# Other step orders for nine units of a Strassen-scheduled decoder block, and a branch sum joined by accumulating transfers

## The chip, the cores and the metric

The kernel runs on one core of a Trainium2 chip. The metric is the time of the kernel on the device, in microseconds, over whole executions; lower is better. A core has a matrix engine (PE), a vector engine (DVE), a scalar engine (ACT), GpSimd (POOL) and SyncE (SP). Each engine works through its own instructions in order, and engines wait for one another by semaphores. SP issues the weight loads, POOL the transfers of everything else; in a row of the profile SPq and POOLq are the queues of these transfers.

## The reference

The input x has 256 tokens of 4096 channels, everything is float32, and one block is computed. Cut to what matters:

```python
h = rmsnorm(x, norm_w)
proj = h @ w_in                        # 4096 -> six parts of 2048 and 8192 gate logits
u_p, z_p, u_c, b_c, c_c, z_c, g_logit = split(proj)
y_pool = pool(u_p, pool_w, pool_scale) * silu(z_p)
y_conv = b_c * shortconv(c_c * u_c, conv_w, conv_b) * silu(z_c)
br = [y_pool @ w_branch[0], y_conv @ w_branch[1]]     # 2048 -> 4096 each
gates = sigmoid(g_logit + gate_b)                     # 2 x 4096
x = x + (gates[0] * br[0] + gates[1] * br[1]) @ w_out # 4096 -> 4096
out = rmsnorm(x, final_norm_w)
```

`pool` takes four groups of 512 channels; each is averaged over a trailing window of 2, 4, 8 or 16 tokens, the token itself is subtracted, and the result is multiplied with a 512 x 512 matrix of its group ("mixing"). `shortconv` is a causal convolution over three tokens.

## The kernel before

**Units and steps.** The outputs of the large products are cut into units of 1024 columns. A unit runs over the rows of its weight matrix in steps of 256 rows by 1024 columns, 1 MB each: 16 steps in an input or output unit, 8 in a branch unit. Every float32 product is made from three passes over values split in a high and a low part (high x high, high x low, low x high). A step is one of two kinds. A direct step ("P") multiplies the four 128-row, 512-column pieces with both halves of the tokens: 24 matmuls of 128 x 512. A Strassen step ("S") makes seven products instead of eight from sums of the pieces: 21 matmuls, in seven groups of three, and needs more of DVE, since it forms four sums of the weights (`parts`) and splits them too. The products of a direct step go into the four banks of PSUM that are called `sums`; those of a Strassen step go into `sums` and the four banks called `shared`. The order of the kinds in a unit is written out as a string (`SEVEN5` is the name of such a string with 7 S, the direct steps first).

**Preparing a step.** SP loads the weights into one of three buffers `raw`. ACT rounds them to high parts, DVE subtracts to get low parts; both go into cells of a `ring` of 15 cells of 512 columns. For a Strassen step DVE first forms the sums in `parts`, which are then split in the same way. Preparation runs up to `AHEAD = 4` steps ahead of PE as the cells come free. In the code, `Step.first` and `Step.rest` issue it, `pump` decides when. A Strassen step is `closing` when it ends its unit; it then fills the banks `sums` in its first three groups and the banks `shared` in the other four.

**The end of a unit.** When a bank is complete, ACT copies it: `evacuate` takes a bank of `sums` into the tile E (Y in some units), `copy_corners` takes a bank of `shared` into J. `corner_sums` combines the four parts of J on DVE, and `combine` adds J to E. It does so on DVE (L61, or L73 with the scale of the norm in `rin`), or, in a unit with `late` set, by two transfers of POOL that accumulate in memory (`gather`, L85); the scale is then applied later. After that comes the unit's epilogue, a list of functions and gaps in a queue. One entry is taken at each "tick", which is every 6 matmuls; `gap(n)` are n ticks without work. So an epilogue runs in the first third of the next unit, between its matmuls, and the engines see its instructions in the place where the tick emitted them.

**The order of units.** cz, cb, cu, cc (the four conv inputs, for c = 0 and then c = 1), pz0, pu0, pz1, pu1 (the pool inputs), eight gate units g0_0, g0_1, g1_1, g0_2, g1_2, g0_3, g1_3, g1_0, then b0_0, b1_0, b0_1, b1_1 and so on to b1_3 (branch units n and c: branch n, columns c), and the outputs o0 to o3. pz1 and g0_0 are hosts: the letter B in their string stands for the step that multiplies the pool input just computed (pu0, pu1) with two band matrices, and M for one group's mixing. In these two units the string `HOST` sets where that stands among their own 16 steps. The epilogues of pu0 and pu1 are empty: E goes into the B step.

**Branch units.** `branch_unit` builds them. b0_c is the pool branch; its result E is multiplied into Y (which holds the first gate) by `mul(Y, E, Y)` during b1_c. In the epilogue of b1_c, which runs during the next b0, E is multiplied with the second gate (`spare()`, the tile `last_pair`), Y is added, and PE transposes the sum (L458) for the output stage. Their left operands, eight of branch 0 and eight of branch 1, lie in `arena` in regions that `place` gives out: four blocks per part for a direct step's operand, seven or eight for a Strassen one's. They are brought in by POOL and split (`Fill`) while the units before run, as regions come free.

Of the kernel before, what the change touches and what calls it, by code (L numbers as in the profile page):

```python
# [10 lines left out]
F32R = mybir.dt.float32r  # L11
# [4 lines left out]
P = 128  # L16
T = 256
D = 4096
HALF = D // 2
NU = 1024  # L20
# [3 lines left out]
KB = 256  # L24

ND, NS, NB = 8, 6, 2
# [5 lines left out]
TAIL = 3  # L32

SIX5 = "PPPPPSPSPSPSPSPS"
SEVEN5 = "PPPPPSPSSPSPSSPS"
FIRST = (0, 1, 8, 2, 9, 3, 10, 11, 4, 12, 13, 5, 14, 6, 15, 7)
OPENED = 12
SEVEN3 = "PPPSPSPSPSPSPSPS"
NINE = "PSPSPSPSSPSPSSPS"
NINE_A = "PSPSSPSPSSPSPSPS"  # L40
HOST = "PPPBPPMMPSPSSPSSPSS"
TEN = "PSPSSPSSPSSPSSPS"
OUT3 = "PSPSPSPSPSPSSPPP"
B0 = "PPPPSPSP"
B1 = "PSPSPSPP"
B1_FIRST = "PPSPSPSP"
B1_LAST = "PSPPSPPP"


@with_exitstack  # L50
def hybrid_block(ctx: ExitStack, tc: tile.TileContext, x, xc, prm, rows_in, w_in, pool_w, w_branch, w_out, out):
    nc = tc.nc
# [4 lines left out]
    def act(dst, src, func=AF.Copy, **kw):  # L57
        return pin(nc.scalar.activation(dst, src, func, **kw))  # L58

    def tt(dst, a, b, op):  # L60
        return pin(nc.vector.tensor_tensor(out=dst, in0=a, in1=b, op=op))  # L61

    def mul(dst, a, b):
        return tt(dst, a, b, ALU.mult)
# [7 lines left out]
    def stt(dst, a, s, b, op0, op1, **kw):  # L72
        return pin(nc.vector.scalar_tensor_tensor(out=dst, in0=a, scalar=s, in1=b, op0=op0, op1=op1, **kw))  # L73
# [7 lines left out]
    def move(dst, src):  # L81
        return pin(nc.gpsimd.dma_start(dst, src))
# [10 lines left out]
    def sb(name, shape, dt=F32):  # L93
        return upper.tile(shape, dt, name=name)

    def blocks(name, shape, dt=F32):
        return const.tile(shape, dt, name=name)

    blocks("front", [P, 96])
    arena = blocks("arena", [P, (4 * ND + 7 * NS + 8 * (NB - 1)) * KB], F32R)  # L100
    ring = blocks("ring", [P, CELLS, 2, NH], F32R)
    E = blocks("E", [P, 2, NU])
    sa = blocks("sa", [P, 8, P])
# [3 lines left out]
    Y = sb("Y", [P, 2, NU])  # L107
# [10 lines left out]
    gates_d = dram.tile([2, 4, P, 2, NU], F32, name="gates_d")  # L118
# [14 lines left out]
    def bias_col(b):  # L133
        return par[:, 80 + b:81 + b]
# [26 lines left out]
    def place(region):  # L161
        kind, i = region
        if kind == "p":
            return 4 * KB * i, 4
        if kind == "q":
            return (4 * ND + 14 + 4 * i) * KB, 4
        if i < NS:
            return (4 * ND + 7 * i) * KB, 7
        return (4 * ND + 7 * NS + 8 * (i - NS)) * KB, 8
# [227 lines left out]
    def shared(i):  # L397
        return PF[i]
# [52 lines left out]
    def transposes(src, done):  # L451
        items = []
        for j in range(4):
            def f(j=j):
                for i in range(2):
                    for t in range(2):
                        c = (2 * j + i) * P
                        pin(nc.tensor.transpose(shared(j)[:, i * T + t * P:i * T + (t + 1) * P],  # L458
                                                src[:, t, c:c + P], ident))
                done(j)  # L460
            items.append(f)
        return items

    def pairs(items):
        return [lambda a=a, b=b: (a(), b()) for a, b in zip(items[::2], items[1::2])]
# [5 lines left out]
    def chan(tile_):  # L471
        return tile_.rearrange("p a n -> p (a n)").rearrange("p (b t) -> p b t", t=T)
# [4 lines left out]
    def gap(n):  # L477
        return [None] * n
# [5 lines left out]
    def make_ops(kinds):  # L484
        return [Operand(k, r) for k, r in kinds]

    x_ops = make_ops([("P" if r[0] == "p" else "S", r) for r in x_regions])
    y_ops = [make_ops([("P", ("p", i)) for i in range(6)] + [("S", ("s", i)) for i in (0, 1)]),
             make_ops([("P", r) for r in (("p", 6), ("p", 7), ("q", 0), ("q", 1), ("q", 2))] +
                      [("S", ("s", i)) for i in (6, 4, 5)])]  # L490
    m_ops = make_ops([("P" if r[0] == "p" else "S", r) for r in x_regions])

    def sequence(text, np_, total, both):
# [24 lines left out]
    def in_unit(name, col, epi, text, **kw):  # L518
        units.append(Unit(name, lambda i: w_in[col // NU, i], seq_x(text), x_ops, epi, scaled=True, **kw))
        units[-1].text = text  # L520
        return units[-1]
# [15 lines left out]
    def silu_y(late):  # L537
        def silu(t):
            act(Y[:, t], Y[:, t], AF.Silu, **(dict(scale=rin[:, t:t + 1]) if late else {}))
        return gap(18 if late else 3) + [lambda: silu(0), None, lambda: silu(1)]  # L540
# [5 lines left out]
    def conv_units(c, first):  # L546
        base = 2 * HALF + c * NU

        def b_epi(u):
            def product(t):  # L550
                stt(E[:, t], E[:, t], rin[:, t:t + 1], Y[:, t], ALU.mult, ALU.mult)
            return gap(18) + [lambda: product(0), None, lambda: product(1), None, lambda: move(g_d[c], E)]

        def c_epi(u):
            def inner(j):
                if j == 3:
                    for i in range(4):
                        act(chan(E)[:, 2 * i:2 * i + 2], bankview(i))

            def outer(j):  # L560
                act(chan(J)[:, 2 * j:2 * j + 2], bankview(j))

            def taps(j):
                v, y = chan(E)[:, 2 * j:2 * j + 2], chan(Y)
                for i in range(2):
                    b = 2 * j + i
                    kb = 8 * c + b
                    act(y[:, b], v[:, i], AF.Identity, scale=tap_col(2, kb), bias=bias_col(kb))
                for s in (1, 2):
                    for i in range(2):  # L570
                        b = 2 * j + i
                        kb = 8 * c + b
                        stt(y[:, b, s:], v[:, i, 0:T - s], tap_col(2 - s, kb), y[:, b, s:], ALU.mult, ALU.add)

            items = [lambda: move(Y, g_d[c])] + gap(6) + pairs(transposes(E, inner)) + gap(5) + pairs(transposes(Y, outer))
            for j, n in enumerate((1, 7, 8, 8)):
                items += gap(n) + [lambda j=j: taps(j)]
            return items + [None, lambda: mul(chan(E), chan(J), chan(Y)), lambda: put(y_d[1, c], chan(E))]

        u = in_unit(f"cz{c}", base + 3 * HALF, lambda u: silu_y(u.late) + (gap(4) + side_items(ND - 1) + side_items(ND - 2) if first else []),  # L580
                    FIRST if first else SEVEN5, dst=Y)
        u.late = not first
        in_unit(f"cb{c}", base + HALF, b_epi, TEN if c else NINE_A).late = True
        u = in_unit(f"cu{c}", base, lambda u: rescale(Y), NINE, dst=Y)
        u.late = True
        in_unit(f"cc{c}", base + 2 * HALF, c_epi, NINE_A).urgent = lambda: mul(E, E, Y)

    def pool_units(c):
        u = in_unit(f"pz{c}", HALF + c * NU, lambda u: silu_y(True) + gap(4) + band_items(c), HOST if c else SEVEN5, dst=Y)
        u.late = True  # L590
        in_unit(f"pu{c}", c * NU, lambda u: [], NINE).urgent = lambda: None

    def band_items(c):
        if c == 0:
# [92 lines left out]
    def gate_unit(n, c):  # L687
        first, final = (n, c) == (0, 0), (n, c) == (1, 0)

        def epi(u):  # L690
# [10 lines left out]
            return items if first or final else items + [lambda: move(gates_d[n, c], E)]  # L701
        text = HOST if first else SEVEN3 if final else TEN
        u = in_unit(f"g{n}_{c}", 6 * HALF + n * D + c * NU, epi, text, dst=Y if first else E)
        u.late = not final

    def spare():
        return last_pair["tile"].rearrange("p (a n) -> p a n", a=2)

    def branch_unit(n, c):
        def epi(u):  # L710
            if n == 0:
                return gap(8) + [lambda: mul(Y, E, Y), None, lambda: c and move(spare(), gates_d[1, c])]
            turned = spare() if c < 3 else Y

            def gated():
                mul(E, E, spare())
                if c == 3:
                    last_pair["stack"].close()
                    open_last(F32R)
                    last_pair["again"] = True  # L720

            def copy(j):
                act(chan(turned)[:, 2 * j:2 * j + 2], bankview(j))

            def stored():
                put(m_d[c], chan(turned))
                merged[c] = now[0] + STORED
            return gap(2) + [gated, None, lambda: add(E, E, Y), None,
                lambda: c < 3 and move(Y, gates_d[0, c + 1])] + gap(3) + pairs(transposes(E, copy)) + [stored]

        text = (B1_LAST if c == 3 else B1 if c else B1_FIRST) if n else B0
        u = Unit(f"b{n}_{c}", lambda i: w_branch[n, c, i], seq_y(text), y_ops[n], epi)
        u.urgent, u.lead = (lambda: None), 3
        units.append(u)

    merged = {}
# [224 lines left out]
    def done(i):  # L961
        steps[i].prepared = True
# [276 lines left out]
```

## Time and profile before

| | |
|---|---|
| runs, median (lowest, highest) | 2361.7 us (2361.68, 2362.04) |
| the profiled execution's own time | 2362.3 us |
| its span in the trace | 2360.3 us |
| granted PE clock in it | 0.999 |
| matmuls; weight loads | 10,436; 10,436 |
| DVE, ACT, POOL instructions | 2430, 1832, 189 |
| moved by transfers | 566.28 MB, mean 240 GB/s |

The span runs from the first to the last instruction of the trace; the execution's own time is 2.0 us longer. The page's busy line gives, for each engine, the time in which it executed something, its share of the span and its instructions; register, branch and DMA-issuing instructions are not in it. PE's ends are modelled, and matmuls overlap, so a stretch in which PE is busy throughout can still hold matmuls that came a little late. For that reason lengths of single steps are read as well: a step begins with its first matmul and ends where the next one begins. Numbers in names (`sums_82`) are of PSUM banks.

### The profile page before, as it was taken

What the parts mean: (1) busy time and instruction counts of PE and PEld (TensorE: products, weight loads), DVE (VectorE), ACT (ScalarE), POOL (GpSimd) and SP (SyncE); (2) the same over time, 40 slices, a digit from 0 to 9 for tenths busy, and PEclk for the clock granted to TensorE, in tenths of its full rate; (3) what the DMA queues carried; (4) which work ended last, traced back from release to release, by engine and by line L of the source; (5) the groups of instructions that cost most, each with busy time, mean ns of one, the idle gap of its engine ahead of it and who ended that gap; (6) DMA issues with size and microseconds to landing.
All of it is one profiled execution on the core that took longest, in us unless ns stands there. A gap on an engine that the chain in (4) does not pass through costs nothing.

```text
span 2360.3 us, 28303 instructions
## 1 busy us (share of the span) xinstructions
PE 2344.8 (99%) x10436; PEld 1939.8 (82%) x10436; DVE 2206.1 (93%) x2430; ACT 1535.1 (65%) x1832; POOL 131.3 (6%) x189
## 2 busy tenths in 40 slices
PE   9999999999999999999999999999999999999998
PEld 7888888888888888888888888888888888888886
DVE  8899989999979979979999999999998798899998
ACT  6666656666666666656767767766665566566665
POOL 0000000000001100100000000001100001000000
PEclk9999999999999999999999999999999999999999
DMA  9667655776756656656887787778766657667877
GB/s 349 234 233 245 221 202 202 253 232 237 230 197 210 235 181 223 231 187 217 253 261 246 259 262 249 249 261 287 250 221 245 251 212 258 245 210 267 259 254 280
DMA packets 93754, 566.28 MB, mean 240 GB/s; under 512 B 10225, under 2 KB 10481, under 8 KB 33201
## 3 DMA queue, kind: packets, MB, share of 16 engines
q1 hardware_dynamic: 69824, 485.39, 56.7%
q0 software_dynamic: 23216, 77.87, 12.9%
q8 instruction: 81, 1.33, 0.2%
q10 hardware_dynamic: 576, 1.24, 0.1%
q14 instruction: 57, 0.46, 0.1%
HBM read 521.46 MB, written 25.17 MB: 232 GB/s over the span
## 4 chain that ended last, share of the span: by engine, by line
PE 93%; DVE 4%; DMA 1%; issue 1%; ACT 1%; SPq 0%; DVEq 0%; ACTq 0%
PE sums L1018 67%; PE shared L1018 24%; DVE ring L61 2%; DVE parts L61 1%; PE shared L672 1%; DMA raw<-in_w_in_dram 1%; PE shared L458 1%; DVE E L61 1%; ACT ring L58 0%; DVE Y L73 0%; DVE J L61 0%; PE shared L648 0%; ACT J L58 0%; DVE E L73 0%; ACT E L58 0%
## 5 line engine op out<-in xcount | busy, mean ns | idle before, releaser
L1018 PE MATMUL sums<-ring,arena 128*128 128x512 f32 x7041 | 1648.4, 390 | 2.5 <-ACT E L58 0.9
L1018 PEld LDWEIGHTS sums<-ring,arena 128*128 128x128 f32 x7041 | 1320.1, 188 | 279.0 <-ACT E L58 2.2
L61 DVE TENSOR_TENSOR ring<-raw,ring 128x1024 fp32r<-128x1024 f32 (+3 forms) x884 | 964.4, 1110 | 92.9 <-ACT ring L58 91.5
L58 ACT ACTIVATE ring<-raw 128x1024 fp32r<-128x1024 f32 (+3 forms) x685 | 787.9, 1190 | 199.9 <-PE sums L1018 79.3
L58 ACT ACTIVATE ring<-parts 128x512 fp32r<-128x512 f32 (+1 forms) x669 | 502.0, 762 | 520.2 <-DVE parts L61 461.4
L1018 PE MATMUL shared<-ring,arena 128*128 128x512 f32 x2217 | 535.4, 389 | 0.0
L61 DVE TENSOR_TENSOR ring<-parts,ring 128x1024 fp32r<-128x1024 f32 (+1 forms) x465 | 515.3, 1150 | 2.9 <-ACT ring L58 2.8
L1018 PEld LDWEIGHTS shared<-ring,arena 128*128 128x128 f32 x2217 | 416.1, 188 | 86.5
L61 DVE TENSOR_TENSOR parts<-parts,raw 128x512 f32<-128x512 f32 x436 | 297.6, 683 | 0.0
L61 DVE TENSOR_TENSOR parts<-raw 128x1024 f32<-128x1024 f32 x218 | 265.2, 1217 | 11.5 <-DMA raw<-in_w_in_dram 6.3
L61 DVE TENSOR_TENSOR J<-J 128x512 f32<-128x512 f32 (+1 forms) x90 | 78.1, 867 | 8.8 <-ACT J L58 6.2
L1018 PE MATMUL sums<-ring,last_pair 128*128 128x512 f32 x336 | 83.0, 389 | 0.0
L1018 PEld LDWEIGHTS sums<-ring,last_pair 128*128 128x128 f32 x336 | 63.0, 188 | 13.2 <-DVE ring L61 0.2
L58 ACT ACTIVATE J<-shared 128x512 f32<-128x512 f32 x128 | 69.1, 603 | 2.2 <-PE shared L1018 0.9
L85 POOL DMA_DIRECT2D E<-J x22 | 26.8, 1459 | 431.3 <-ACT ring L58 315.5
L1018 PE MATMUL shared<-ring,side 128*128 128x512 f32 x207 | 50.7, 389 | 0.0
L1018 PE MATMUL shared<-ring,last_pair 128*128 128x512 f32 x192 | 46.1, 389 | 0.0
L1018 PEld LDWEIGHTS shared<-ring,side 128*128 128x128 f32 x207 | 38.9, 188 | 8.1
L58 ACT ACTIVATE E<-sums 128x512 f32<-128x512 f32 x76 | 42.0, 596 | 4.0 <-PE sums L1018 1.8
L1018 PEld LDWEIGHTS shared<-ring,last_pair 128*128 128x128 f32 x192 | 36.0, 188 | 7.5
L85 POOL DMA_DIRECT2D Y<-J x12 | 14.7, 1455 | 247.6 <-issue 121.7
L672 PE MATMUL shared<-ring 128*128 128x512 f32 x96 | 22.1, 389 | 0.0
(140 smaller groups left out, 639.3 us busy)
## 6 DMA issues: line engine op xcount, KB each, us to landing
raw<-in_w_in_dram SPq DMA_DIRECT2D x318, 1024.0 KB, 4.9
raw<-in_w_branch_dram SPq DMA_DIRECT2D x64, 1024.0 KB, 4.8
raw<-in_w_out_dram SPq DMA_DIRECT2D x64, 1024.0 KB, 5.1
E<-J POOLq DMA_DIRECT2D x22, 512.0 KB, 8.8
E<-in_rows_dram POOLq DMA_DIRECT2D x14, 512.0 KB, 9.6
Y<-J POOLq DMA_DIRECT2D x12, 512.0 KB, 9.7
gates_d<-E POOLq DMA_DIRECT2D x6, 1024.0 KB, 6.2
y_d<-E POOLq DMA_DIRECT2D x8, 512.0 KB, 7.7
```

What stands on the lines that cost most here:

```text
L58: return pin(nc.scalar.activation(dst, src, func, **kw))
L61: return pin(nc.vector.tensor_tensor(out=dst, in0=a, in1=b, op=op))
L85: return pin(nc.gpsimd.dma_start(dst, src, accum_op=ALU.add))
L458: pin(nc.tensor.transpose(shared(j)[:, i * T + t * P:i * T + (t + 1) * P], src[:, t, c:c + P], ident))
L672: pin(nc.tensor.matmul(o, a, b, start=(k, i) == (0, 0), stop=(k, i) == (3, 2)))
L1018: pin(nc.tensor.matmul(ps, lhs, rhs, start=n == 0, stop=n == u.total[b] - 1))
```

## The change

- **Fewer Strassen steps in cz1 and pz0.** They take `SIX5` (six S) instead of `SEVEN5` (seven).
- **Hosts.** `HOST` has one S more, and B stands one step earlier, behind two direct steps instead of three.
- **pu0 and pu1.** A new string `NINE_P` with the same nine S, but a direct step at the end.
- **Branch units.** b0_1, b0_2 and b0_3 take `B0_MORE` with three S instead of two, and close with one. They become `late`: the sum E + J is made by POOL's transfers instead of DVE, and they lose the rule by which their last step holds back preparation (`lead`). Their epilogue waits longer: `mul(Y, E, Y)` comes 19 ticks into b1 instead of 8, and the load of the second gate, which stood behind it, stands 10 ticks in. b1_3 takes `B1` (three S) instead of `B1_LAST` (two). b0_0 keeps `B0`, b1_0 keeps `B1_FIRST`.
- **Transposes.** In the epilogues of b1_0 to b1_2 the gap before them is 4 instead of 3.
- **Room.** The branch operands get other regions (`place` has two more kinds), since one more of each branch is held as a Strassen operand; `arena` grows by two blocks, and the scratch memory for the descriptors of POOL's transfers is halved.

```diff
-SEVEN5 = "PPPPPSPSSPSPSSPS"
...
+NINE_P = "PSPSSPSPSSPSSPSP"
-HOST = "PPPBPPMMPSPSSPSSPSS"
+HOST = "PPBPPMMPSSPSSPSSPSS"
...
-B1_LAST = "PSPPSPPP"
+B0_MORE = "PPPPSSPS"
...
-    arena = blocks("arena", [P, (4 * ND + 7 * NS + 8 * (NB - 1)) * KB], F32R)
+    arena = blocks("arena", [P, (4 * ND + 7 * NS + 8 * (NB - 1) + 2) * KB], F32R)
...
-    y_ops = [make_ops([("P", ("p", i)) for i in range(6)] + [("S", ("s", i)) for i in (0, 1)]),
-             make_ops([("P", r) for r in (("p", 6), ("p", 7), ("q", 0), ("q", 1), ("q", 2))] +
-                      [("S", ("s", i)) for i in (6, 4, 5)])]
+    y_ops = [make_ops([("P", ("p", i)) for i in range(5)] + [("S", r) for r in (("t", 0), ("s", 0), ("s", 1))]),
+             make_ops([("P", r) for r in (("p", 7), ("q", 0), ("q", 1), ("q", 2), ("q", 3))] +
+                      [("S", ("u", i)) for i in (2, 0, 1)])]
...
-                    FIRST if first else SEVEN5, dst=Y)
+                    FIRST if first else SIX5, dst=Y)
...
-        u = in_unit(f"pz{c}", HALF + c * NU, lambda u: silu_y(True) + gap(4) + band_items(c), HOST if c else SEVEN5, dst=Y)
+        u = in_unit(f"pz{c}", HALF + c * NU, lambda u: silu_y(True) + gap(4) + band_items(c), HOST if c else SIX5, dst=Y)
         u.late = True
-        in_unit(f"pu{c}", c * NU, lambda u: [], NINE).urgent = lambda: None
+        in_unit(f"pu{c}", c * NU, lambda u: [], NINE_P).urgent = lambda: None
...
             if n == 0:
-                return gap(8) + [lambda: mul(Y, E, Y), None, lambda: c and move(spare(), gates_d[1, c])]
+                if c:
+                    return gap(10) + [lambda: move(spare(), gates_d[1, c])] + gap(8) + [lambda: mul(Y, E, Y)]
+                return gap(8) + [lambda: mul(Y, E, Y)]
...
-                lambda: c < 3 and move(Y, gates_d[0, c + 1])] + gap(3) + pairs(transposes(E, copy)) + [stored]
-
-        text = (B1_LAST if c == 3 else B1 if c else B1_FIRST) if n else B0
+                lambda: c < 3 and move(Y, gates_d[0, c + 1])] + gap(4) + pairs(transposes(E, copy)) + [stored]
+
+        text = (B1 if c else B1_FIRST) if n else B0_MORE if c else B0
...
-        u.urgent, u.lead = (lambda: None), 3
+        u.late = n == 0 and c > 0
+        if not u.late:
+            u.urgent, u.lead = (lambda: None), 3
...
-    nc = _bacc.Bacc("TRN2", target_bir_lowering=False, num_devices=1, dynamic_dma_scratch_size=4096)
+    nc = _bacc.Bacc("TRN2", target_bir_lowering=False, num_devices=1, dynamic_dma_scratch_size=2048)
```

The first place is DVE at the end of cz1, from the last sums of its last but one Strassen step to the first step of the next unit. `parts<-raw` begins a Strassen step, `ring<-parts` ends it, `ring<-raw` alone is a direct step, the rows with Y are taps of the convolution in an epilogue. Before:

```order
L61 TENSOR_TENSOR ring<-parts,ring 128x2x512 x2
L61 TENSOR_TENSOR parts<-raw 128x1024
L61 TENSOR_TENSOR ring<-raw,ring 128x512
L61 TENSOR_TENSOR parts<-parts,raw 128x512
L61 TENSOR_TENSOR ring<-raw,ring 128x512 x2
L61 TENSOR_TENSOR parts<-parts,raw 128x512
L73 SCALAR_TENSOR_TENSOR Y<-E,par,Y 128x255 x2
L73 SCALAR_TENSOR_TENSOR Y<-E,par,Y 128x254 x2
L61 TENSOR_TENSOR ring<-parts,ring 128x2x512 x2
L61 TENSOR_TENSOR E<-J,Y 128x2048
L61 TENSOR_TENSOR ring<-raw,ring 128x2x512 x2
L61 TENSOR_TENSOR parts<-raw 128x1024
```

and of the changed kernel:

```order
L61 TENSOR_TENSOR ring<-parts,ring 128x2x512 x2
L61 TENSOR_TENSOR ring<-raw,ring 128x2x512 x2
L61 TENSOR_TENSOR parts<-raw 128x1024
L61 TENSOR_TENSOR ring<-raw,ring 128x512
L61 TENSOR_TENSOR parts<-parts,raw 128x512
L61 TENSOR_TENSOR ring<-raw,ring 128x2x512
L61 TENSOR_TENSOR parts<-parts,raw 128x512
L73 SCALAR_TENSOR_TENSOR Y<-E,par,Y 128x255 x2
L73 SCALAR_TENSOR_TENSOR Y<-E,par,Y 128x254 x2
L61 TENSOR_TENSOR ring<-parts,ring 128x512 x2
L61 TENSOR_TENSOR ring<-parts,ring 128x2x512
L61 TENSOR_TENSOR E<-J,Y 128x2048
```

Before, two Strassen steps follow each other directly at the end; now a direct step, the second row, stands between the last two. The taps and the join of the unit (`E<-J,Y`) keep their places around the last step.

The second place is PE at the end of b0_1: before, the last groups of its second Strassen step and the first of the direct step that ends the unit (the four banks then come a second time, as its last groups):

```order
L1018 MATMUL shared_87<-ring,arena 128x512 x3
L1018 MATMUL shared_86<-ring,arena 128x512 x3
L1018 MATMUL shared_88<-ring,arena 128x512 x3
L1018 MATMUL sums_84<-ring,arena 128x512 x3
L1018 MATMUL sums_82<-ring,arena 128x512 x3
L1018 MATMUL sums_84<-ring,arena 128x512 x3
L1018 MATMUL sums_81<-ring,arena 128x512 x3
L1018 MATMUL sums_83<-ring,arena 128x512 x3
```

and of the changed kernel its last step and the first groups of b1_1:

```order
L1026 MATMUL sums_82<-ring,arena 128x512 x3
L1026 MATMUL sums_81<-ring,arena 128x512 x3
L1026 MATMUL sums_84<-ring,arena 128x512 x3
L1026 MATMUL shared_85<-ring,arena 128x512 x3
L1026 MATMUL shared_87<-ring,arena 128x512 x3
L1026 MATMUL shared_86<-ring,arena 128x512 x3
L1026 MATMUL shared_88<-ring,arena 128x512 x3
L1026 MATMUL sums_82<-ring,arena 128x512 x3
L1026 MATMUL sums_84<-ring,arena 128x512 x3
L1026 MATMUL sums_81<-ring,arena 128x512 x3
L1026 MATMUL sums_83<-ring,arena 128x512 x3
```

The banks `sums_82`, `sums_81` and `sums_84` are now completed by the first three groups of the last step, and the `shared` banks by the last four; before, the four `sums` banks were completed by the very last groups and the `shared` banks eight groups earlier.

The third place is POOL in the branch units, the piece of the difference from b0_1 to b0_2:

```order
 L82 DMA sb<-m_d 128x512
 L82 DMA sc<-m_d 128x512
+L85 DMA E<-J 128x2x512 x2
 L82 DMA last_pair<-gates_d 128x2048
 L82 DMA Y<-gates_d 128x2048
 L82 DMA m_d<-last_pair 512x1x256 x2
+L85 DMA E<-J 128x2x512 x2
 L82 DMA last_pair<-gates_d 128x2048
```

POOL now issues the two accumulating transfers of J into E ahead of the load of the second gate, in each of these units.

More of the change, by code (lines that the diff above doesn't have):

```diff
@@ L166, in place @@
             return (4 * ND + 14 + 4 * i) * KB, 4
+        if kind == "t":
+            return (4 * ND - 12) * KB, 8
+        if kind == "u":
+            return (4 * ND + 30 + 7 * i) * KB, 7 + i // 2
         if i < NS:
```

## The prediction

> **What bounds the kernel now.** I read the page first, its busy line.
>
> ```profile
> span 2360.3 us, 28303 instructions
> PE 2344.8 (99%) x10436; PEld 1939.8 (82%) x10436; DVE 2206.1 (93%) x2430; ACT 1535.1 (65%) x1832; POOL 131.3 (6%) x189
> ```
>
> PE is busy 99% of the span, so the kernel can only get shorter by fewer matmuls, or by the few microseconds in which PE waits. DVE at 93% is the next engine, and a Strassen step puts work on it. So the two questions are where PE waits, and whether DVE keeps ahead of it. The second view is the busy time by stretch, over whole units and stages (columns: PE, weight loads, DVE, ACT, POOL, clock, DMA share, GB/s).
>
> ```profile
> 176.03:256.95 80.92, 80.92 (x358) 67.00 (x357) 78.57 (x87) 51.72 (x62) 3.07 (x3) 1.00 0.69 234
> 1056.13:1112.74 56.61, 56.61 (x258) 46.88 (x257) 56.18 (x64) 40.79 (x55) 1.56 (x2) 1.00 0.64 231
> 1192.98:1273.22 80.24, 80.24 (x355) 66.44 (x354) 80.17 (x90) 56.60 (x69) 5.30 (x6) 1.00 0.79 258
> 1594.18:1676.46 82.28, 82.28 (x364) 68.13 (x363) 74.94 (x87) 55.70 (x66) 10.24 (x15) 1.00 0.83 275
> 1933.31:1977.95 44.64, 44.31 (x203) 36.30 (x202) 37.46 (x37) 26.93 (x36) 4.72 (x8) 1.00 0.71 246
> 1977.95:2020.25 42.30, 42.30 (x186) 34.98 (x187) 39.76 (x44) 27.23 (x30) 2.67 (x5) 1.00 0.70 248
> ```
>
> The first row is unit cu0, nine Strassen steps of 21 matmuls and seven direct ones of 24: 357 in 80.92 us, 0.2267 us each at full clock, so 4.76 us for a Strassen step and 5.44 for a direct one. The second row is the stage of g0_0 behind its mixing, the third the gate unit g1_1: there DVE has 0.43 and 0.07 us left, yet PE does not wait. The others are the last input unit g1_0, b0_3 and b1_3.
>
> The third view is what PE waited for in the whole span.
>
> ```profile
> PE sums L1018 <- ACT E L58: 0.9, 2, 0.6
> PE shared L458 <- DVE E L61: 0.8, 1, 0.8
> PE sums L1018 <- DVE ring L766: 0.8, 1, 0.8
> PE sums L1018 <- DVE ring L61: 0.7, 2, 0.4
> ```
>
> L766 is the start, which the change leaves alone. The other three are waits for E to be emptied by ACT, for the transposes' operand, and for ring cells from DVE. Matmuls overlap, so this view undercounts. I price each by the length of its step instead, against a step of the same kind without a wait (same columns; here the weight loads alone).
>
> ```profile
> 395.23:399.99 4.76, 3.94 (x21) 1.00 0.49 203
> 419.05:424.52 5.47, 3.87 (x21) 1.00 0.86 316
> 747.85:753.18 5.33, 3.86 (x21) 1.00 0.73 285
> 753.18:758.79 5.61, 4.43 (x24) 1.00 0.72 261
> 1755.01:1761.21 6.20, 4.32 (x23) 1.00 0.92 383
> 1761.21:1766.80 5.59, 4.61 (x25) 1.00 0.66 245
> 1772.24:1780.53 8.29, 6.08 (x40) 1.00 0.60 214
> 1858.76:1865.89 7.13, 6.08 (x40) 1.00 0.62 223
> 1944.19:1951.60 7.41, 6.08 (x40) 1.00 0.58 179
> 1972.02:1977.95 5.93, 4.32 (x24) 1.00 0.80 247
> 1977.95:1983.52 5.57, 4.61 (x25) 1.00 0.41 166
> ```
>
> **The change, part by part.** *Matmuls.* Strassen steps gained: one in each of the two units that host bands and mixing (pz1, g0_0), one in b0_1, b0_2, b0_3, and one in b1_3. Lost: one in cz1 and one in pz0. That is 6 - 2 = 4 steps of 21 instead of 24: 12 matmuls x 0.2267 = **-2.72 us**, all on the path.
>
> *Waits that go.* (a) cz1 and pz0 had seven Strassen steps and closed late: 5.47 - 4.76 = 0.71, 5.33 - 4.76 = 0.57, and 5.61 - 5.44 = 0.17 in the direct step behind pz0. What DVE did there stands in its timeline (start, length, tiles), then one row from the end of g0_0, and two from a gate unit for the price of a step:
>
> ```profile
> 418.80 2.36 DVE L61 TENSOR_TENSOR ring<-parts,ring 128x1024 fp32r<-128x1024 f32 x2
> ...
> 1104.18 2.35 DVE L61 TENSOR_TENSOR ring<-parts,ring 128x1024 fp32r<-128x1024 f32 x2
> ...
> 1396.91 1.21 DVE L61 TENSOR_TENSOR parts<-raw 128x1024 f32<-128x1024 f32 x1
> ...
> 1403.26 2.42 DVE L61 TENSOR_TENSOR ring<-raw,ring 128x512 fp32r<-128x512 f32 x3
> ```
>
> The closing step of cz1 began at 419.05 and DVE finished it at 421.16, 2.11 us late; a closing step needs its last sum in its third of seven groups, 1.4 us in, hence the 0.71. A Strassen step takes DVE 1403.26 - 1396.91 = 6.35 us, a direct one, three roundings in one row, 2.42. One fewer frees 3.9 us of DVE, more than the 2.11: the wait goes, **-1.45 us**. Next to be late is nothing, since the unit behind then starts with DVE 1.8 us ahead.
>
> For the next parts, groups of instructions (busy time, mean ns of one):
>
> ```profile
> L61 DVE TENSOR_TENSOR sa<-sa 128x128 f32<-128x128 f32 x68 | 16.6, 286 | 0.8 <-ACT sa L58 0.2
> L61 DVE TENSOR_TENSOR arena<-sa,arena 128x1024 fp32r<-128x1024 f32 x2 | 2.4, 1220 | 0.0
> L61 DVE TENSOR_TENSOR E<-E,J 128x2048 f32<-128x2048 f32 x8 | 18.3, 2284 | 0.9 <-ACT E L58 0.9
> L73 DVE SCALAR_TENSOR_TENSOR E<-J,rin,E 128x1024 f32<-128x1024 f32 x10 | 12.4, 1280 | 0.1
> L58 ACT ACTIVATE E<-sums 128x512 f32<-128x512 f32 x76 | 42.0, 596 | 4.0 <-PE sums L1018 1.8
> ```
>
> (b) In b0_1 to b0_3 PE transposes E, and waits for DVE's sum of the two branches: 8.29 - 7.13 = 1.16 and 7.41 - 7.13 = 0.28. The transposes move one tick back, 6 matmuls or 1.36 us, and what DVE does before them stays: **-1.44 us**.
>
> (c) b0_3 ended with a direct step, so b1_3 had to wait for ACT to empty the banks: 5.93 - 5.44 and 5.57 - 5.44, together 0.62. A unit that closes with Strassen fills its E banks in its first three groups and leaves four more groups, 2.7 us, in which ACT has only four copies to make; at 596 ns each they take 2.4: **-0.62 us**.
>
> *Waits that stay.* b0_0 and b1_0 keep their steps, and b0_1 its late banks: 0.76 + 0.15 at 1755 to 1767. One operand of b0_0 is now split as a Strassen one: four small subtractions and a wider rounding, 4 x 0.29 + 1.22 = 2.4 us of DVE at most. g1_0 just ahead has 7.3 us of DVE idle, so I cost it at nothing; without that cover it is up to 2.4.
>
> *New direct ends.* pu0 and pu1 now close with a direct step, so pz1 and g0_0 may wait for the banks as at the three ends above: between 0 and 0.91 us each, and not below nothing, since PE does not wait at those ends today. No operand is filled in those units, and the copies of the shared banks come a step earlier, so ACT should be free; I take 0.15 each, **+0.3 us**. The band step one place earlier needs E complete 10.9 us (two direct steps) into the unit; behind the last bank come two joins, a rounding and a difference, some 7 us in all, so it costs nothing.
>
> *DVE behind mixing.* There is one Strassen step more: DVE loses 6.35 - 4.76 = 1.59 us against PE. The closing step of g0_0 began at 1112.74 - 4.76 = 1107.98, and DVE had finished it at 1106.53, 1.45 ahead; with the 0.43 idle that leaves 0.3 ahead, and a wait starts only at 1.4 behind. The gate units that follow are as full as they were and start 1.2 us worse, inside the same margin. Cost nothing; if the cover is gone, up to 0.7 at each of eight closing steps. [...]
>
> *Branch units.* b0_1 to b0_3: +3.9 us of DVE, less the joining sum of 2.28 that POOL's transfer takes over; b0_3 has 7.2 us of DVE idle. b1_3: 39.8 + 3.9 = 43.7 us of DVE in 41.6 of PE, 2.1 too much; it starts far ahead, since its first direct step (1977.95) is ready at 1971.99:
>
> ```profile
> 1969.70 2.29 DVE L61 TENSOR_TENSOR ring<-raw,ring 128x2048 fp32r<-128x2048 f32 x1 [4.05 <-ACT ring L58]
> ```
>
> So nothing, or up to 2.1 without that lead.
>
> *Sum.* -2.72 - 1.45 - 1.44 - 0.62 + 0.3 = **-5.9 us**. The profiled execution took 2362.3 us, which gives 2356.4; it stood 0.6 above the median of 2361.7, so for the median **2355.8 us**.
>
> **The rivals.** 0.2%, or 4.7 us, is about what a measurement of this kernel can tell from no change: the bounds are 2357.0 and 2366.4.
>
> *New waits eat the margin.* Only 1.2 us lie between the forecast and 2357.0. Two direct ends at 0.91 and b1_3 at 2.1 would make 2355.8 - 0.3 + 1.8 + 2.1 = 2359.4; eight closing steps of gate units at 0.7, 2361.4. For it: ACT was late at the ends of this kind with E as target, and DVE is full in the gates. Against it: b1_1, b1_2 and b1_3 also end with direct steps, and the list of waits has none there; g1_1 runs unbroken at 80.17 us of DVE in 80.24. Chance 0.29.
>
> *The transposes still wait.* If DVE's sum slips as far as the transposes do, (b) does not come: 2357.2. Against it, DVE's order up to that sum is unchanged. Chance 0.07.
>
> *Slower: the joining transfer comes late.* In b0_1 to b0_3 POOL adds J into E, and the product of E and Y, now 19 ticks (25.8 us) into the next unit, stands in DVE's queue ahead of the rounding of later steps; behind it everything PE needs would stop. The transfers in hand (count and landing, us min/median/max, and their issue in g1_1, which began at 1192.98):
>
> ```profile
> L85 POOL DMA_DIRECT2D E<-J x22: 1174/1462/1766, 181.5 to 2274.9; - x22
> DMA to landing us min/median/max: 5.5/8.8/14.9
> 1199.14 2.43 POOL L85 DMA_DIRECT2D E<-J  x2 [54.67 <-ACT ring L58]
> ```
>
> Issue 6.2 us in, the second 1.2 later, and at worst 14.9 to land: 22.3, so 3.5 us to spare. It decides from a landing of 18.4 us, and past a lead of DVE of 3 us, which I estimate from the 6.0 that it has at b1_3, every microsecond counts three times: at 30 us it is 3 x 8.6 - 5.9, 2381.6. Half the descriptor scratch for POOL's transfers is a reason for it; against it, POOL is 6% busy, and the row was taken beside a DVE at 93%. Chance 0.10.
>
> **How the numbers follow.** Forecast 0.54, with a range of its own of 2354.6 (the waits that stay, 0.91, and the 0.3 for the direct ends go as well) to 2357.0. Within 0.2%: 0.29 + 0.07 = 0.36. Slower 0.10. The range reaches over the first two rivals to 2361.4, and leaves out the late transfer and a little below 2354.6.
>
> **What would show it.** Right: 10,424 matmuls; the closing steps of cz1 and pz0 at 4.76 us; the direct steps with transposes at 7.1; no wait for E at the start of b1_3; pz1 and g0_0 beginning with 5.44 us; E<-J landing under 15 us. Wrong: PE waiting for ring cells in g0_0 to g1_3, for banks behind pu0 and pu1, or DVE idle before Y<-E,Y in b1_1 to b1_3.

## The result, and the profile after

The changed kernel takes 2357.04 us (median of 14 runs, 2356.25 to 2358.07) against 2362.12 (14 runs): 5.1 us less, a ratio of 0.9978 with a 95% interval of 0.9970 to 0.9986. The profiled execution took 2356.82 us with a span of 2354.7, 5.6 less than before. First the page's busy line, then what PE waited for in the whole span.

```profile
span 2354.7 us, 28337 instructions
PE 2340.7 (99%) x10424; PEld 1938.7 (82%) x10424; DVE 2217.8 (94%) x2454; ACT 1542.9 (66%) x1841; POOL 139.0 (6%) x195
```

```profile
PE shared L873 <- DVE warm L869: 1.1, 1, 1.1
PE sums L1026 <- ACT E L58: 1.1, 1, 1.1
PE sums L1026 <- DVE ring L774: 0.8, 1, 0.8
```

There are 12 matmuls less. The waits for the transposes' operand and for ring cells are gone from the list; beside the kernel's start (the rows of L873 and L774) one wait is left, for ACT to empty E, and at 1.1 us it is longer than the two before it together. The steps that answer to the prediction's table (length, weight loads, clock, DMA share, GB/s):

```profile
419.72:424.48 4.76, 3.94 (x21) 1.00 0.59 224
748.40:753.16 4.76, 3.94 (x21) 1.00 0.62 220
753.16:758.60 5.44, 4.50 (x24) 1.00 0.54 193
834.08:839.52 5.44, 4.50 (x24) 1.00 0.29 122
1013.11:1018.55 5.44, 4.50 (x24) 1.00 0.47 191
1711.63:1718.30 6.67, 4.32 (x24) 1.00 0.95 364
1754.51:1759.95 5.44, 4.51 (x24) 1.00 0.95 378
1770.83:1777.17 6.34, 5.33 (x32) 1.00 0.47 167
1777.17:1783.53 6.36, 5.33 (x32) 1.00 0.85 293
1972.81:1978.25 5.44, 4.50 (x24) 1.00 0.61 231
```

Rows one and two are the closing steps of cz1 and pz0, both without a wait; three to five the first steps behind pz0, pu0 and pu1. Row six is the last step of b0_0: 6.67 against 5.44 without a wait, the place that got worse. Before it was

```profile
1713.18:1718.81 5.63, 4.32 (x23) 1.00 0.95 365
```

Row seven is the last step of b1_0, which waited 0.76 before. Rows eight and nine are the two steps of b0_1 over which the transposes now spread; each is 0.9 longer than a plain direct step, as in b0_2 and b0_3, and that is the transposes themselves. The last row is the start of b1_3.

Unit by unit, after less before: cz1 -0.05, cb1 -0.09, pz0 +0.11, pu0 -0.17, pz1 -0.70, g0_0 -0.69, b0_0 **+1.04**, b1_0 -0.74, b0_1 -1.89, b0_2 -0.65, b0_3 -1.34, b1_3 -0.82, o2 +0.37, the others within 0.03; together -5.6.

What stood ahead of PE at the end of b0_0 is in ACT's timeline (start, length, tiles, idle time before and what ended it):

```profile
1715.76 1.49 ACT L58 ACTIVATE ring<-raw 128x1536 fp32r<-128x1536 f32 x1 [1.29 <-DMA raw<-in_w_branch_dram]
1717.15 0.61 ACT L58 ACTIVATE arena<-sb 128x512 fp32r<-128x512 f32 x1
1717.67 2.04 ACT L58 ACTIVATE E<-sums 128x512 f32<-128x512 f32 x4
```

ACT stood idle for 1.29 us until weights of b1_0 landed, rounded them, copied a branch operand, and only then emptied the banks. The place of b1_0's first matmul without a wait would have been 1711.63 + 5.44 = 1717.07; the first bank was free at about 1718.3, hence 1.23.

### The profile page after: what moved, and what is told of

Its sections match the earlier page's. It is cut to its first block, busy times and chain, and to the rows that moved or that the text cites. A ratio compares the mean times of both kernels' runs of the same rounds, so it can differ in the third digit from the quotient of the medians.

```text
span 2354.7 us, 28337 instructions
## 1 busy us (share of the span) xinstructions
PE 2340.7 (99%) x10424; PEld 1938.7 (82%) x10424; DVE 2217.8 (94%) x2454; ACT 1542.9 (66%) x1841; POOL 139.0 (6%) x195
## 4 chain that ended last, share of the span: by engine, by line
PE 97%; DVE 1%; DMA 0%; ACT 0%; issue 0%; DVEq 0%; SPq 0%; ACTq 0%
PE sums L1026 70%; PE shared L1026 25%; PE shared L676 1%; PE shared L462 1%; DVE ring L61 1%; DMA raw<-in_w_branch_dram 0%; DVE parts L61 0%; DMA raw<-in_w_in_dram 0%; ACT ring L58 0%; DVE arena L61 0%; PE shared L652 0%; DVE J L61 0%; ACT E L58 0%; PE shared L653 0%; PE shared L655 0%
## 5 line engine op out<-in xcount | busy, mean ns | idle before, releaser
L61 DVE TENSOR_TENSOR ring<-raw,ring 128x1024 fp32r<-128x1024 f32 (+2 forms) x887 | 962.2, 1104 | 70.4 <-ACT ring L58 69.5
L58 ACT ACTIVATE ring<-parts 128x512 fp32r<-128x512 f32 (+1 forms) x683 | 510.4, 761 | 510.2 <-DVE parts L61 438.3
L1026 PE MATMUL shared<-ring,arena 128*128 128x512 f32 x2241 | 541.1, 389 | 0.0
L61 DVE TENSOR_TENSOR ring<-parts,ring 128x1024 fp32r<-128x1024 f32 (+1 forms) x475 | 524.5, 1146 | 8.7 <-ACT ring L58 8.7
L61 DVE TENSOR_TENSOR parts<-parts,raw 128x512 f32<-128x512 f32 x444 | 303.3, 683 | 0.0
L1026 PE MATMUL sums<-ring,last_pair 128*128 128x512 f32 x306 | 76.2, 389 | 0.0
L85 POOL DMA_DIRECT2D E<-J x28 | 34.2, 1463 | 479.5 <-ACT ring L58 300.1
L1026 PE MATMUL shared<-ring,last_pair 128*128 128x512 f32 x216 | 51.9, 389 | 0.0
L58 ACT ACTIVATE E<-sums,rin 128x512 f32<-128x512 f32 x20 | 13.0, 689 | 13.9 <-PE sums L1026 13.9
```

Source lines behind the costliest of these rows:

```text
L85: return pin(nc.gpsimd.dma_start(dst, src, accum_op=ALU.add))
L1026: pin(nc.tensor.matmul(ps, lhs, rhs, start=n == 0, stop=n == u.total[b] - 1))
```

## The experiments

All are the changed kernel with one edit, or two where that is said. Their times stand beside its own 2357.04; the kernel before took 2362.2 to 2362.5 in the same sessions.

**The same program again.**

> The changed kernel once more, for what differs between executions of one program. Theory: the first step of the kernel and the wait behind b0_0 vary with the landing of loads: b0_0 between 42.2 and 43.4, cz0 between 88.9 and 90.1, o2 80.92 or 81.29; all other units within 0.1 us. Rival: they are fixed by the program and come out as before, and the differences in the other runs were made by their edits.

2356.59 us (9 runs, ratio 0.9975, 0.9965 to 0.9985). In the profile the last step of b0_0 is shorter, o2 has no wait, and cz0 is 0.28 longer:

```profile
1711.83:1718.08 6.25, 4.32 (x23) 1.00 0.92 343
```

So b0_0's wait was 1.2 in one execution and 0.8 in the other; in three runs below whose edits lie only behind b0_0 it is 0.0, 1.1 and 1.1. The +0.37 in o2 differs between two executions of one program, so it can't be put down to the change. In the other executions below cz0 lies between 88.9 and 90.1. Differences under half a microsecond in the totals say nothing here; the lengths of single steps do.

**The transposes a tick earlier.**

```diff
-... gates_d[0, c + 1])] + gap(4) + pairs(transposes(E, copy)) + [stored]
+... gates_d[0, c + 1])] + gap(3) + pairs(transposes(E, copy)) + [stored]
```

> The changed kernel with the transposes of b1_0 to b1_2 a tick earlier again (gap 3). Theory: the later tick is what took the waits for E away; in the changed kernel E is ready at 1775.14 us, 0.46 ahead of the transposes in b0_1, and 1.37 ahead in b0_2 and 1.36 in b0_3. A tick of 1.36 us earlier, b0_1 waits about 0.9 us and the other two less than 0.1: 43.30 becomes about 44.2 us for b0_1, the total +0.9. Rival: the waits went because the b0 units now begin with DVE further ahead, and the tick is idle: +0.0.

2358.53 us (ratio 0.9984, 0.9975 to 0.9993). b0_1 is 44.48 us, 1.18 more than in the changed kernel, and b0_2 and b0_3 are 0.10 and 0.13 longer: +1.4 in the three, of which 0.14 is at b0_1's start and belongs to the wait at the end of b1_0 below. The wait for E is back in the list, and the step with the transposes is 8.27 long:

```profile
PE shared L462 <- DVE E L61: 0.8, 1, 0.8
```

```profile
1712.45:1717.92 5.47, 4.32 (x24) 1.00 0.96 353
1771.20:1779.47 8.27, 6.09 (x40) 1.00 0.59 212
```

The tick is what took these waits away. The first of the two rows is b0_0's last step in the same execution: no wait, though every instruction up to there is that of the changed kernel. ACT's rows tell why, the weights had landed when ACT came to them, 2.9 us into the step. In the first profile of the changed kernel ACT stood idle for 1.29 us until they landed, and began to round them only 4.1 us into the step (1715.76 against 1711.63). In the rows here no idle time stands ahead of it:

```profile
1715.37 1.49 ACT L58 ACTIVATE ring<-raw 128x1536 fp32r<-128x1536 f32 x1
1716.77 0.61 ACT L58 ACTIVATE arena<-sb 128x512 fp32r<-128x512 f32 x1
1717.29 2.04 ACT L58 ACTIVATE E<-sums 128x512 f32<-128x512 f32 x4
```

The end of b1_0 then waits 0.63 instead. What is lost at this place moves between two steps.

**Seven Strassen steps again in cz1 and pz0.**

```diff
-FIRST if first else SIX5 ...  HOST if c else SIX5
+FIRST if first else SEVEN5 ...  HOST if c else SEVEN5
```

> The changed kernel with seven Strassen steps in cz1 and pz0 as before. By the sum: six matmuls less, -1.36 us, and the late closing steps return, 0.71 + 0.57, with 0.17 in pu0 and 0.09 in cb1: +0.2 in all, which is no change; dropping the two steps was worth nothing by itself. Rival: the 4 us of DVE work that come back are passed on to pu0 and pz1, whose last sums are now done only 0.4 us ahead, and cost 0.5 to 1.5 us more there.

2359.09 us (ratio 0.9985, 0.9976 to 0.9995). The rival holds, a little above its 0.5 to 1.5 and all in pu0: the closing steps are 5.43 and 5.32, about as before the change, and another 1.59 is lost at a Strassen step late in pu0:

```profile
813.85:820.19 6.34, 3.86 (x21) 1.00 0.46 164
```

```profile
815.98 2.35 DVE L62 TENSOR_TENSOR ring<-parts,ring 128x1024 fp32r<-128x1024 f32 x2
```

DVE finished that step's sums at 818.33, 4.5 us into it. In the changed kernel the same pair of instructions stands at

```profile
812.91 2.35 DVE L61 TENSOR_TENSOR ring<-parts,ring 128x1024 fp32r<-128x1024 f32 x2
```

1.6 us into the step, which begins at 813.68, in time for its later groups. Giving up the two steps is a wash in its own units (with seven they are +0.07 together) and pays behind them. Before the change pz0 had seven too and pu0 lost only 0.17; what differs there is pu0's order (`NINE`, now `NINE_P`), so it is the new order that needs the room, as far as these two profiles can tell.

**b0_0: weights rounded behind the bank copies.** In `after_group`:

```diff
+        if u.name == "b0_0" and st in u.steps[-2:]:
+            state["limit"] = state["now"] + (3 if st is u.steps[-2] else 2)
```

> The changed kernel, with the rounding of the weights of the step b1_0 2S emitted behind the copies of b0_0's four banks on ACT, not ahead of them. Theory: the 1.23 us that PE waits behind b0_0 come from ACT, which stands 1.29 us waiting for these weights and then rounds them for 1.49 us ahead of the first copy. Without it b0_0 is 1.2 us shorter (42.2); the Strassen step 2S of b1_0 was ready 2.93 us ahead of its use and is now ready some 2.5 to 4 us later, so 0 to 1 us may come back there: total -1.2 to 0. Rival: the copy of a branch operand into arena, which also stands ahead of the banks, is the cause: b0_0 stays at 43.4 or loses less than 0.3.

2358.24 us, 1.2 more than the changed kernel, where -1.2 to 0 was expected. b0_0's end has no wait, as the theory has it, but that of b1_0 has 1.48, more than the 0 to 1 allowed for.

```profile
1711.71:1717.15 5.44, 4.51 (x25) 1.00 0.86 328
1753.37:1760.29 6.92, 4.32 (x23) 1.00 0.92 330
```

**b0_0: no operand copy ahead of the banks.** `pop_fill` advances no operand during b0_0's last step.

> The changed kernel, with no branch operand advanced during the last step of b0_0, so that ACT's copy into arena (0.61 us) comes behind the copies of the banks. Theory (ACT waits for late weights): b0_0 loses just the copy, 0.6 us, total -0.6. Rival (the operand's copy and what it moves is the whole cause): b0_0 loses 1.0 to 1.2 us.

2356.74 us. The step is 6.42 long, 0.25 less; neither size came. In this execution ACT stood 1.53 us for the weights:

```profile
1716.08 1.49 ACT L58 ACTIVATE ring<-raw 128x1536 fp32r<-128x1536 f32 x1 [1.53 <-DMA raw<-in_w_branch_dram]
1717.47 2.04 ACT L58 ACTIVATE E<-sums 128x512 f32<-128x512 f32 x4
```

They were rounded 0.32 later than in the first profile, and the copy's 0.61 less 0.32 is about the 0.25 seen. That fits the theory's size less a later landing, but two executions of the changed kernel differ by 0.4 at this step, so one profile does not show it.

**b0_0 closing with a Strassen step.**

```diff
-B0 = "PPPPSPSP"
+B0 = "PPPPSPPS"
```

> The changed kernel with the second Strassen step of b0_0 at its end (direct steps at places 5 and 6), joined on DVE. Theory: the 1.23 + 0.18 us behind b0_0 are the copies of the four sums banks, which stand on ACT behind a weight load that lands late; a closing Strassen step fills these banks 2.7 us before the unit's end, so both go: -1.4, whenever the load lands. Rival (the wait only moves on, since DVE and ACT are full here): b0_0 gains and b1_0 or the start of b0_1 gives 0.6 us or more back.

2358.02 us. The rival holds: b0_0 loses its 1.23, and b1_0 becomes 2.30 longer, in its second Strassen step and at its end:

```profile
1738.72:1744.51 5.79, 3.87 (x21) 1.00 0.50 181
1754.71:1761.60 6.89, 4.32 (x24) 1.00 0.93 334
```

**The join on DVE again.**

```diff
-        u.late = n == 0 and c > 0
+        u.late = False
```

> The changed kernel, but b0_1 to b0_3 join J into E on DVE (2.28 us each) as before, and hold back preparation in their last step. Theory (the join is off the path; the transfer only buys DVE time): in b1_1 and b1_2 the least lead of a Strassen step is 2.05 and 2.11 us and goes to about -0.2, which costs nothing; in b1_3 it is 0.16 and goes to -2.1, 0 to 0.6 us of wait there. Total 0 to +0.6. Rival (the transfer join is what carries the third Strassen step): waits in the first Strassen step of each b1 unit, +1.5 or more.

2362.85 us (ratio 1.0002, 0.9993 to 1.0011): the whole gain is gone, and neither theory had this cause. b1_1 and b1_2 are unchanged; the end of b1_3 is 4.25 longer and the first step of o0 1.69.

```profile
2009.46:2019.15 9.69, 4.32 (x24) 1.00 0.66 252
2019.15:2026.28 7.13, 5.77 (x25) 0.77 0.72 280
```

```profile
2015.35 0.95 ACT L58 ACTIVATE arena<-sa 128x896 fp32r<-128x896 f32 x1 [3.00 <-DVE sa L61]
2016.20 1.89 ACT L58 ACTIVATE ring<-raw 128x2048 fp32r<-128x2048 f32 x1
2018.00 0.61 ACT L58 ACTIVATE arena<-sb 128x512 fp32r<-128x512 f32 x1
2018.52 2.03 ACT L58 ACTIVATE E<-sums 128x512 f32<-128x512 f32 x4
```

ACT waited 3.0 us for DVE's sums of an output operand, copied that operand, rounded weights, copied another operand, and then emptied E. A `late` unit also holds back the fetching of further operands for 14 ticks after its join (`hush`, set in `combine`), another unit not at all; so these copies had moved ahead of the banks. In the changed kernel one copy alone stands among them, and ACT waits for no operand:

```profile
2012.45 0.60 ACT L58 ACTIVATE E<-sums 128x512 f32<-128x512 f32 x1
2012.95 0.62 ACT L58 ACTIVATE arena<-sb 128x512 fp32r<-128x512 f32 x1
2013.47 1.62 ACT L58 ACTIVATE E<-sums 128x512 f32<-128x512 f32 x3
```

**The join on DVE, operands held back as before the edit.**

```diff
-        u.late = n == 0 and c > 0
+        u.late = False
-        hush[0] = now[0] + (HUSH if u.late else 0)
+        hush[0] = now[0] + (HUSH if u.late or u.name in ("b0_1", "b0_2", "b0_3") else 0)
```

> As join_on_dve, but with the operands of the output stage held back after the join as long as in the changed kernel (14 ticks), so that ACT's and POOL's other work keeps its order and DVE gets nothing but the three joins of 2.28 us. Theory (the +5.9 us of join_on_dve came from the operand copies, which the join by transfer holds back as a side effect and which otherwise stand on ACT ahead of b1_3's banks): b1_3 is back at 41.5 to 42.3 us, the total 0 to +0.8 against the changed kernel. Rival (DVE cannot take 2.28 us more in b1_3): b1_3 and o0 stay 3 us or more longer.

2356.81 us (ratio 0.9979, 0.9969 to 0.9988), the changed kernel's time. This kernel differs from the changed one by three additions on DVE in place of the six transfers, and by the rule on the last step (`lead`) that comes back with `late` off; b1_3's end and o0's start are as there:

```profile
2008.92:2014.36 5.44, 4.50 (x24) 1.00 0.76 294
2014.36:2019.82 5.46, 4.50 (x24) 1.00 0.69 227
```

So the join by transfers itself is worth nothing measurable. The two kernels with the join on DVE differ in the hold alone, by 6.0 us: what `late` sets beside the join, the time for which operands are held back, is worth that there. The transfers without the hold were not run.

**pu0 and pu1 closing with a Strassen step.** Their string is `NINE` again.

> The changed kernel with the old string of pu0 and pu1, which closes with a Strassen step. Theory: the direct end costs nothing and brings little: before the change the band operand was split 5.01 us ahead of its use, behind another step's 2.3 us; one direct step (5.44) earlier it is still 1 to 2 us ahead, total 0 to +0.2. Rival (the direct end is what lets the band stand a step sooner): the two band steps wait for E, about 1 us each, +2.

2357.34 us. The two band steps are 0.31 and 0.33 longer, a third of the rival's price and above the theory's; the 0.3 more in the total is inside the noise. The first of the two, 3.65 in the changed kernel:

```profile
845.24:849.20 3.96, 3.62 (x32) 1.00 0.08 17
```

**The band behind three direct steps.**

```diff
-HOST = "PPBPPMMPSSPSSPSSPSS"
+HOST = "PPPBPMMPSSPSSPSSPSS"
```

> The changed kernel with B behind three direct steps and one direct step between B and mixing, the same eight Strassen steps behind. Theory: mixing needs the band's result, which is ready 4.9 us ahead with two direct steps between; with one it is about 0.55 us late, so PE waits 0.3 to 1.1 us in each host: +0.6 to +2.2, all at M. Rival: what bounds the hosts is DVE behind mixing, and the band's place does not matter: 0.

2356.89 us; the hosts keep their 98.08 us, the first mixing step has its length, and DVE had split the band's result for it by 856.97, 2.5 us ahead:

```profile
859.48:864.92 5.44, 4.51 (x24) 1.00 0.54 193
855.74 1.23 DVE L61 TENSOR_TENSOR ring<-E,ring 128x1024 fp32r<-128x1024 f32 x1 [0.78 <-ACT ring L58]
```

The rival holds: the eighth Strassen step of the hosts does not need the band's earlier place. The expectation took the whole lead of 4.9 us as fixed behind the band; with one direct step between, half of it is still there.

**Room on DVE in b1_0.** The edit of "weights behind the bank copies", and:

```diff
-B1_FIRST = "PPSPSPSP"
+B1_FIRST = "PPPSPPSP"
```

> As b00_weights_later, with two Strassen steps in b1_0 instead of three (3.9 us less for DVE, three matmuls more, +0.68). Theory (the waits from b0_0 to b0_1 move on because DVE is full there, by fills and three plus two Strassen steps): with the room neither b0_0 (42.2) nor the end of b1_0 waits, b1_0 is 42.2: total against the changed kernel -1.41 + 0.68, -0.5 to -0.9. Rival (ACT's order alone makes these waits): b1_0 waits at its end still, 0.6 us or more, total 0 or above.

2357.03 us, no change, where -0.5 to -0.9 was expected. From b0_0 to b0_1 it is as the theory has it: both units 42.16 long without a wait, 0.73 less than in the changed kernel's first profile and 0.4 less than in its second. But o0's last step waited 1.23 for an operand (the list of waits names DVE's write into arena, with 0.9), since, as the next run bears out, three matmuls more shift the ticks behind. Two things changed at once in b1_0: DVE has 3.9 us less to do, and a direct step stands third, where the first Strassen step was. Which of them takes the waits away was not separated, nor was b1_0 run so without the other edit.

**The same, with the last operands of o0 a tick sooner.**

```diff
-                merged[c] = now[0] + STORED
+                merged[c] = now[0] + STORED - (c == 3)
```

> As b10_two_strassen, and the last operands of the output stage brought in one tick sooner, so that in o0 DVE finishes the last of them 2.36 us earlier, ahead of the low parts of a direct step and not behind them. Theory (in b10_two_strassen the 0.73 won from b0_0 to b0_1 was given back as 1.23 at the last step of o0, where this operand came late because three more matmuls shift the ticks by half of one): o0 is back at 84.8 us and the total 0.7 below the changed kernel, some 2355.9 against 2356.6 to 2357.0. Rival: the wait at the end of o0 moves to another step there, or the 0.7 is lost elsewhere: 2356.6 or more.

2356.24 us (7 runs, ratio 0.9973, 0.9961 to 0.9984), between the theory's 2355.9 and the rival's 2356.6. None of the three places waits any more:

```profile
1712.08:1717.52 5.44, 4.50 (x24) 1.00 0.89 299
1754.24:1759.68 5.44, 4.50 (x24) 1.00 0.77 267
2094.04:2098.80 4.76, 3.94 (x21) 1.00 0.50 177
```

That is the lowest median of all kernels here, 0.35 to 0.8 below the changed kernel's two; their intervals largely overlap, so it is not shown to be faster than that one.

## Why the prediction was right, point by point

The forecast was -5.9 us for the profiled execution and 2355.8 for the median. The span became 5.6 shorter, and the profiled execution took 2356.82 where 2356.4 was forecast; the median, 2357.04, is 1.2 above its forecast. Most of that 1.2 is the step from one to the other: the prediction put the median 0.6 below the profiled execution, from three runs of the kernel before, and here it lies 0.2 above it. So 2357.04 is 0.04 above the bound of 2357.0, outside the forecast's own range and inside the range that takes in the first two rivals. The mechanism of those rivals did not come: PE waits for no ring cells in g0_0 to g1_3, for no banks behind pu0 and pu1, and for no operand of the transposes.

That the sum came within 0.3 is in part luck. Against the forecast, the direct ends cost 0.3 less and (a) brought 0.1 more; (b) brought 0.25 less, the waits from b0_0 to b0_1 grew by 0.15, and o2 was 0.37 longer, which the second execution does not have.

- *Matmuls, -2.72.* As summed. pz1 and g0_0 are 0.70 and 0.69 shorter, a Strassen step each; DVE's lead at the end of g0_0 was forecast at 0.3 us. The closing step begins at 1111.19 - 4.76 = 1106.43, and DVE's last pair behind

```profile
1103.70 2.35 DVE L61 TENSOR_TENSOR ring<-parts,ring 128x1024 fp32r<-128x1024 f32 x2
1191.43:1271.67 80.24, 80.24 (x356) 66.44 (x354) 80.17 (x90) 56.51 (x69) 5.29 (x6) 1.00 0.80 258
```

  ends at 1106.05, 0.38 ahead. The second row is g1_1 after the change, unbroken with DVE at 80.17 of 80.24 us.
- *Waits that go, (a) -1.45.* 4.76, 4.76 and 5.44: gone to the last hundredth, and 0.09 at the start of cb1 with them. But the account is short: it looked at the closing steps and the unit's first step only. With seven steps in pz0 the new order of pu0 would have waited 1.59 late in pu0, so most of what giving them up is worth is a wait that the prediction did not name.
- *(b) -1.44.* The waits are gone, and by the tick, as the run without it shows; but 1.19 came, not 1.44. The term was read from one step. The transposes now spread over two, and the third and fourth steps of b0_1 to b0_3 together went from 39.29 to 38.10 us.
- *(c) -0.62.* Gone. With a closing Strassen step in b0_1 to b0_3 there is no wait at the start of b1_1 to b1_3; this is read from the lengths, and no run took the closing step back.
- *New direct ends, +0.3.* 0.0; both hosts begin with 5.44. The end is worth having: with the old string the band steps wait 0.3 each.
- *Waits that stay.* The size held and the place did not. Before the change the steps from the end of b0_0 to the start of b0_1 held 1.25 us of waits: the 0.91 of the prediction, and 0.34 at the end of b0_0 and the start of b1_0 that it left out. After it they held 1.4, in the second execution 1.1 and in the run with the tick taken back 1.0, so the new Strassen operand of b0_0, put at nothing, cost nothing that can be told from that. But the waits were to stay at the end of b1_0, with DVE as the engine to watch and 7.3 us of its idle time as cover; instead b0_0 became 1.04 longer and b1_0 0.74 shorter, and the engine was ACT: the rounding of weights that land late and an operand copy stand ahead of its copies of the banks. Whether the change itself makes these weights land later, the runs do not show: the kernel before has one profile here, without that wait. Rounding the weights later only moved the wait to b1_0; the one edit that left none took a Strassen step from b1_0.
- *Branch units.* b1_3 runs without a wait, with DVE full as forecast:

```profile
1972.81:2014.29 41.48, 41.48 (x184) 34.35 (x183) 41.14 (x46) 29.92 (x36) 5.14 (x8) 1.00 0.87 279
DMA to landing us min/median/max: 5.7/9.6/14.3
```

- *The late transfer.* The second row is the landing of the six new transfers: at most 14.3 us, under the 15 of the forecast and the 18.4 from which it would have decided. The rival looked at the wrong thing, though: the join without transfers takes the same time, so the transfers were not needed for the third Strassen step. What `late` does beside them, holding operand copies back, was worth 6 us with the join on DVE, and the prediction did not name it.

## What to carry to other kernels

ACT empties the matrix engine's banks here in the order of its own instructions, so read what stands ahead of those copies at each unit's end: 1.29 us of waiting for a load came ahead of a wait of 1.23 us on PE at the end of b0_0, and 3.00 us of waiting for DVE's sums, in the run with the join on DVE, ahead of one of 4.1 at the end of b1_3, though ACT is busy for only 66% of the changed kernel's span. Where an engine is nearly full over several units, as DVE is from b0_0 to b0_1 here (busy 41.66 of 43.39, 40.69 of 41.65 and 39.55 of 43.30 us), removing a wait at one step moved it to the next (1.23 us at the end of b0_0, then 1.48 at that of b1_0); giving up an expensive step there, or ahead of it as in pz0, can be worth what it costs or more. Price a wait over the steps that can take it up, not at one. And when one flag sets two things, undo them one at a time: the visible one (who does the addition) was worth nothing here, the one beside it 6 us.

## What the runs showed of the hardware

In the run with the join on DVE a wait of 4.1 us on PE cost more than itself. Behind it the granted clock was 0.52 in one stretch of 2 us and 0.63 in the next (columns: PE, clock, DMA share, GB/s):

```profile
2017.00:2019.00 2.00, 0.00 (x0) 1.00 0.14 41
2019.00:2021.00 2.00, 1.85 (x4) 0.52 0.92 373
2021.00:2023.00 2.00, 2.00 (x7) 0.63 0.82 258
2023.00:2025.00 2.00, 2.00 (x11) 1.00 0.91 385
```

In the first row PE stands idle with the clock still at 1.00, and in the last the clock is back. The two rows between hold 2 x (1 - 0.52) + 2 x (1 - 0.63) = 1.70 us of lost clock, and that is the 1.69 us by which o0's first step was longer. Waits of 1.23 us (the changed kernel, at the end of b0_0) and 1.59 us (seven Strassen steps again, in pu0) had no such stretch behind them: in their own steps and in what followed, 1718.30 to 1723.91 and 820.20 to 826.00, the clock was 1.00.

The other surprise is how much a load's landing matters at one place. The changed kernel and the run with the tick taken back have the same instructions up to there. ACT began to round the weights 4.13 and 2.92 us into b0_0's last step, and the step took 6.67 and 5.47 us: the rounding began 1.21 later in the changed kernel, and the step was 1.20 longer. In its second execution the same step took 6.25.
